# Split SiLU-multiply on one core: each partition owns 128 adjacent rows in place of 8 rows of every block

## The chip, the cores and the metric

The kernel runs on one core of a Trainium2 chip. The metric is device time in microseconds for one execution, the median of several runs.

## The reference

```python
x = np.random.randn(32, 512, 2048).astype(np.float32)

half_dim = x.shape[-1] // 2
x1, x2 = x[..., :half_dim], x[..., half_dim:]
silu_x1 = x1 * (1 / (1 + np.exp(-x1)))
return (silu_x1 * x2).astype(np.float32)      # (32, 512, 1024)
```

There are 32 x 512 = 16,384 rows. A row of x is 2048 floats (8 KB), a row of the output 1024 floats (4 KB). All of x is 134.2 MB, all of the output 67.1 MB.

## The kernel before

The rows are flattened to a 16,384 x 2048 matrix and cut into 16 tiles of 1024 rows. In a tile each of the 128 partitions holds K = 8 rows. Tile i is the i-th block of 1024 adjacent rows; `view` (line 51) cuts it with `"(p k) d -> p k d"`, so partition p holds rows 8p to 8p + 7 of that block. `view` serves the loads (from `x_flat`) and the stores (to `out_flat`) alike.

There are two input buffers `xt` (128 x 8 x 2048) and two output buffers `ot` (128 x 8 x 1024); tile i uses buffer i % 2 of each. For a tile:

- `load(i)` issues one DMA of 8.39 MB from sync's queue (SP; queue q1 in the profile).
- `compute(i)` runs SiLU on the scalar engine (ACT, line 103), in place on the first half of each row in `xt`, and the multiply on the vector engine (DVE, line 109) from `xt` into `ot`. Steady tiles do this in one instruction each over 128 x 8192 elements; tile 0 is cut into four pieces of two rows, the last tile into two pieces of four rows.
- `store(i)` issues one DMA of 4.19 MB from the scalar engine's queue (q10); tile 0 is stored in five pieces that take every fourth or every second partition (`OPENING`), the last tile in two.

All DMAs pass through `move` (line 86), so they carry line 87 in the profile. Loads 0 and 1 go out first. After that the loop issues load i + 2 and the store of tile i in an order that alternates every four tiles (`load_first`); `after` keeps that order without a semaphore wait. Load i + 2 waits for the multiply of tile i, which is the last reader of its buffer; the multiply of tile i waits for the store of tile i - 2, which frees its `ot`. The schedule of ACT and DVE is written out by hand (`manual_schedule`), and `implied` removes dependencies that other waits already cover. At the end sync waits for all the transfers but the last (`settle_all_but`).

Of the kernel before, what the change touches and what calls it, by code (L numbers as in the profile page):

```python
# [1 line left out]

# [4 lines left out]


@with_exitstack
def kernel(  # L10
    ctx: ExitStack,
    tc: tile.TileContext,
    x: bass.AP,
    out: bass.AP,
):


    nc = tc.nc
    P = nc.NUM_PARTITIONS

    x_flat = x.flatten_outer_dims()
    out_flat = out.flatten_outer_dims()
    num_rows, in_cols = x_flat.shape
    half = in_cols // 2
    dt = x_flat.dtype

    K = 8
    KC_EDGE = 2
    KS = 4
    OPENING = [  # L30
        (slice(0, None, 4), slice(0, 2)),
        (slice(2, None, 4), slice(0, 4)),
        (slice(2, None, 4), slice(4, None)),
        (slice(0, None, 4), slice(2, None)),
        (slice(1, None, 2), slice(None)),
    ]
    PLAN = [K] * (num_rows // (P * K))

    pool = ctx.enter_context(tc.tile_pool(name="pool", bufs=1))
    xts = [pool.tile([P, K, in_cols], dt, name=f"xt{b}") for b in range(2)]  # L40
    ots = [pool.tile([P, K, half], dt, name=f"ot{b}") for b in range(2)]

    plan = []
    row = 0
    for k in PLAN:
        plan.append((row, k))
        row += P * k
    assert row == num_rows
    n_tiles = len(plan)

    def view(flat, i):
        row0, k = plan[i]
        return flat[row0:row0 + P * k].rearrange("(p k) d -> p k d", k=k)

    ctx.enter_context(tc.manual_schedule(engines={mybir.EngineType.Activation, mybir.EngineType.DVE}))

    sent = []
    loads, stores, silus, muls = {}, {}, {}, {}

    def implied(later, earlier, reason):  # L60
        for x in later:
            for y in earlier:
                tc.declare_no_dep(x, y, reason=reason)

    def earlier(done, i):
        return [ins for j in range(i % 2, i, 2) for ins in done[j]]

    def after(later, first):
        tc.add_manual_dep(
            later,  # L70
            first.name,
            mybir.DependencyInfo(mybir.DependencyClass.NoSync, mybir.DependencyReason.DATA),
            reason="order in which the transfers take their semaphores",
        )

    def settle_all_but(n):
        rest = nc.sync.nop(nofuse=True)
        for ins in sent[:-n]:
            tc.add_manual_dep(
                rest.ins,  # L80
                ins.name,
                mybir.DependencyInfo(mybir.DependencyClass.Sync, mybir.DependencyReason.DATA),
                reason="sync sees each earlier transfer land before the last ones",
            )

    def move(queue, out, in_):
        ins = queue.dma_start(out=out, in_=in_).ins  # L87
        sent.append(ins)
        return ins

    def load(i):
        loads[i] = [move(nc.sync, xts[i % 2][:], view(x_flat, i))]
        if i >= 2:
            implied(loads[i], earlier(loads, i), "the multiplies that this load awaits came after those loads")
            implied(loads[i], earlier(silus, i), "the multiplies that this load awaits came after those activations")

    def compute(i, ot, kc):
        xt = xts[i % 2]
        silus[i], muls[i] = [], []
        for c in range(0, K, kc):  # L100
            ks = slice(c, c + kc)
            silus[i].append(
                nc.scalar.activation(  # L103
                    out=xt[:, ks, :half],
                    in_=xt[:, ks, :half],
                    func=mybir.ActivationFunctionType.Silu,
                ).ins
            )
            muls[i].append(nc.vector.tensor_mul(out=ot[:, ks], in0=xt[:, ks, :half], in1=xt[:, ks, half:]).ins)  # L109
        implied(muls[i], loads[i], "each multiply awaits an activation that came after the load")  # L110
        if i >= 2:
            implied(silus[i], earlier(silus, i), "the load that this activation awaits came after those activations")
            implied(silus[i], earlier(muls, i), "the load that this activation awaits came after those multiplies")
            implied(muls[i], earlier(muls, i), "the store that this multiply awaits came after those multiplies")

    def store(i, ot, pieces):
        ov = view(out_flat, i)
        stores[i] = [move(nc.scalar, ov[ps, ks], ot[ps, ks]) for ps, ks in pieces]

    ALL = slice(None)  # L120
    load(0)
    load(1)
    for i in range(n_tiles):
        ot = ots[i % 2]
        last = i == n_tiles - 1
        compute(i, ot, KC_EDGE if i == 0 else KS if last else K)
        pieces = [(ALL, ALL)]
        if i == 0:
            pieces = OPENING
        elif last:  # L130
            pieces = [(ALL, slice(c, c + KS)) for c in range(0, K, KS)]
        load_first = i // 4 % 2
        if load_first and i + 2 < n_tiles:
            load(i + 2)
        store(i, ot, pieces)
        if load_first and i + 2 < n_tiles:
            after(stores[i][0], loads[i + 2][0])
        if not load_first and i + 2 < n_tiles:
            load(i + 2)
            after(loads[i + 2][0], stores[i][-1])  # L140
    settle_all_but(1)


# [1 line left out]
_INS = ['x']  # L145
_OUTS = [((32, 512, 1024), 'float32')]


# [23 lines left out]
```

## Time and profile before

| | us |
|---|---|
| median of 3 runs | 470.65 |
| lowest and highest run | 470.65 and 471.86 |
| profiled execution, own time | 471.83 |
| profiled execution, span | 470.1 |
| ACT busy | 114.1 |
| DVE busy | 139.3 |

| transfers | number | MB | median us from issue to landing |
|---|---|---|---|
| loads `xt<-in_x_dram` | 16 | 134.22 | 42.1 |
| whole-tile stores `out_dram<-ot` | 14 | 58.7 | 49.2 |
| pieces of the first and last tile's stores | 7 | 8.4 | 9.4 to 28.1 |

The span is the time from the first to the last instruction of the profiled execution; its own time is the time measured for that same execution as a whole. The profile counts how long the packets of each DMA queue kept the 16 DMA engines busy, as a share of the span. A load in steady state takes 42 us from issue to landing because its packets share the engines with those of a store.

### The profile page before, as it was taken

How to read it: one execution, taken by the hardware profiler on the slowest of the kernel's cores; microseconds unless marked ns; L12 is line 12 of the kernel's file. 1: busy time of each engine (PE TensorE's matmuls, PEld its weight loads, DVE VectorE, ACT ScalarE, POOL GpSimd, SP SyncE). 2: the span in 40 equal slices, each digit the busy share in tenths (PEclk: the TensorE clock that was granted, in tenths of full speed). 3: DMA queues.
4: the chain of work that ended last, by engine and by line, in shares of the span. 5: the costliest groups of instructions: out<-in, count | busy, mean ns of one | idle time of the engine just before them, and what ended most of it. 6: DMA issues, size and time to landing. Idle time of an engine off the chain costs nothing.

```text
span 470.1 us, 157 instructions
## 1 busy us (share of the span) xinstructions
DVE 139.3 (30%) x20; ACT 114.1 (24%) x21; POOL 0.2 (0%) x4
## 2 busy tenths in 40 slices
DVE  0070614307042070520605116060150702507061
ACT  1052305050040501405014050230503205032060
POOL 0000000000000000000000000000000000000000
DMA  8999999999999999999999999999999999999997
GB/s 357 446 468 424 402 441 404 415 480 402 446 402 485 407 421 427 485 407 402 443 446 443 407 443 488 393 415 443 482 407 446 404 429 460 407 446 421 424 425 336
DMA packets 4880, 201.33 MB, mean 428 GB/s; under 512 B 592, under 2 KB 592, under 8 KB 592
## 3 DMA queue, kind: packets, MB, share of 16 engines
q1 hardware_dynamic: 2304, 134.22, 66.2%
q10 hardware_dynamic: 2576, 67.11, 33.1%
HBM read 134.22 MB, written 67.11 MB: 428 GB/s over the span
## 4 chain that ended last, share of the span: by engine, by line
DMA 80%; DVE 14%; ACT 2%; DVEq 1%; issue 0%; SPq 0%
DMA out_dram<-ot 62%; DMA xt<-in_x_dram 18%; DVE ot L109 14%; ACT xt L103 2%; DVEq L167 1%; SPq L87 0%; DVEq L109 0%
## 5 line engine op out<-in xcount | busy, mean ns | idle before, releaser
L109 DVE TENSOR_TENSOR ot<-xt 128x8192 f32<-128x8192 f32 (+2 forms) x20 | 139.3, 6984 | 320.5 <-DMA out_dram<-ot 180.1
L103 ACT ACTIVATE xt<-xt 128x8192 f32<-128x8192 f32 (+2 forms) x20 | 112.8, 5661 | 339.7 <-DMA xt<-in_x_dram 339.7
L103 ACT ACT_TABLE_LOAD x1 | 1.3, 1283 | 0.7 <-PEq L156 0.7
L156 POOL MEMSET const-bfloat16-1.0<- 128x1 bf16 x1 | 0.1, 102 | 0.0
L156 POOL MEMSET const-uint8-127<- 128x1 uint8 x1 | 0.1, 102 | 0.0
L156 POOL MEMSET const-float32-0.0<- 128x1 f32 x1 | 0.1, 99 | 0.2 <-issue 0.2
L156 POOL MEMSET const-float32-1.0<- 128x1 f32 x1 | 0.1, 99 | 0.0
## 6 DMA issues: line engine op xcount, KB each, us to landing
out_dram<-ot ACTq DMA_DIRECT2D x14, 4096.0 KB, 49.2
out_dram<-ot ACTq DMA_DIRECT2D x3, 2048.0 KB, 9.4
out_dram<-ot ACTq DMA_DIRECT2D x2, 512.0 KB, 17.3
out_dram<-ot ACTq DMA_DIRECT2D x1, 768.0 KB, 28.1
xt<-in_x_dram SPq DMA_DIRECT2D x16, 42.1
out_dram<-ot ACTq DMA_DIRECT2D x1, 256.0 KB, 10.9
```

Of the source, the lines that this page charges most:

```text
L103: nc.scalar.activation(out=xt[:, ks, :half], in_=xt[:, ks, :half], func=mybir.ActivationFunctionType.Silu,).ins
L109: muls[i].append(nc.vector.tensor_mul(out=ot[:, ks], in0=xt[:, ks, :half], in1=xt[:, ks, half:]).ins)
L156: nc = _bacc.Bacc("TRN2", target_bir_lowering=False, num_devices=1)
L167: with _tile.TileContext(nc) as tc:
```

## The change

Partition p now owns rows 128p to 128p + 127 of x and of the output, and tile i is the i-th group of eight rows of each partition. The tiles keep their shape, number and order, and eight adjacent rows still go to a partition in each tile. The list `plan` falls away, since the new view needs only the tile's number.

```diff
-    PLAN = [K] * (num_rows // (P * K))
+    n_tiles = num_rows // (P * K)
...
-    plan = []
-    row = 0
-    for k in PLAN:
-        plan.append((row, k))
-        row += P * k
-    assert row == num_rows
-    n_tiles = len(plan)
-
     def view(flat, i):
-        row0, k = plan[i]
-        return flat[row0:row0 + P * k].rearrange("(p k) d -> p k d", k=k)
+        return flat.rearrange("(p t k) d -> t p k d", p=P, k=K)[i]
```

Rows of x that one partition reads for tile i:

| | first row | bytes in one run | from one partition's run to the next partition's | from a tile to the next, same partition |
|---|---|---|---|---|
| before, x | 1024 i + 8 p | 64 KiB | 64 KiB | 8 MiB |
| after, x | 128 p + 8 i | 64 KiB | 1 MiB | 64 KiB |
| before, out | 1024 i + 8 p | 32 KiB | 32 KiB | 4 MiB |
| after, out | 128 p + 8 i | 32 KiB | 512 KiB | 32 KiB |

## The prediction

> **What bounds the kernel now.** I read the page from the top: busy shares, then the DMA queues, then the chain that ended last, then the waits, and last the work in stretches of one steady length.
>
> ```profile
> span 470.1 us, 157 instructions
> DVE 139.3 (30%) x20; ACT 114.1 (24%) x21; POOL 0.2 (0%) x4
> DMA packets 4880, 201.33 MB, mean 428 GB/s; under 512 B 592, under 2 KB 592, under 8 KB 592
> q1 hardware_dynamic: 2304, 134.22, 66.2%
> q10 hardware_dynamic: 2576, 67.11, 33.1%
> DMA out_dram<-ot 62%; DMA xt<-in_x_dram 18%; DVE ot L109 14%; ACT xt L103 2%; DVEq L167 1%; SPq L87 0%; DVEq L109 0%
> ```
>
> No compute engine is busy for a third of the span. The two queues (q1 the loads, q10 the stores) together take 66.2 + 33.1 = 99.3% of all 16 DMA engines' time, and the chain is 80% DMA. The chain names the stores most often only because each multiply waits for its `ot` buffer; the engines under it also carry the loads.
>
> The queue lines give a price per byte. Loads: 0.662 x 470.1 = 311.2 us for 134.22 MB, or 431 GB/s. Stores: 0.331 x 470.1 = 155.6 us for 67.11 MB, also 431 GB/s. They give the packet size too. There are 16 loads and 21 stores, and 37 x 16 engines = 592, the number of packets under 512 B, so these are the small ones that end each transfer. Of the 2304 on q1, 256 are such, and 2048 carry data: 134.22 MB / 2048 = 65,536 B. One load is 128 packets, one for each partition's eight adjacent rows. A packet takes at most 16 x 311.2 us / 2048 = 2.43 us.
>
> The stretches show how steady this is. Columns: the stretch and its length, busy time on DVE, ACT and POOL, the granted clock, the DMA share, GB/s.
>
> ```profile
> 0.00:60.00 60.00, 17.52 (x5) 15.62 (x6) 0.20 (x4) 1.00 0.99 419
> 60.00:118.00 58.00, 17.45 (x3) 14.06 (x2) 0.00 (x0) 1.00 0.99 425
> 118.00:176.00 58.00, 17.39 (x2) 14.06 (x2) 0.00 (x0) 1.00 1.00 434
> ...
> 350.00:408.00 58.00, 17.38 (x2) 14.06 (x2) 0.00 (x0) 1.00 1.00 434
> 408.00:470.10 62.10, 17.45 (x3) 14.15 (x3) 0.00 (x0) 1.00 0.96 414
> ```
>
> Two tiles (25.17 MB) pass in each 58 us, at 434 GB/s and a share of 1.00. Only the start and the drain are lower. The waits show the slack on the other side:
>
> ```profile
> ACT xt L103 <- DMA xt<-in_x_dram: 339.7, 16, 22.4
> DVE ot L109 <- DMA out_dram<-ot: 180.1, 9, 20.8
> DVE ot L109 <- ACT xt L103: 140.4, 7, 24.6
> ```
>
> ACT waits about 22 us for each load, DVE about 20 us for a store or for ACT. Nothing that shortens compute could help, and anything that lengthens a packet lengthens the span almost one for one, since the engines have 0.7% idle to give.
>
> **What the change removes and adds: addresses only.** The list `plan` is Python and costs no instruction. Loads stay 16 and stores 21; the SBUF side, the semaphores, the order of issue and all ACT and DVE work stay as they are. A partition still reads 8 x 8 KB = 64 KiB in one run and writes 8 x 4 KB = 32 KiB in one run, so I expect the 4880 packets again. All this costs nothing, with no cover needed.
>
> What moves is where the runs lie in memory. In x, neighbouring partitions lie 64 KiB apart before and 128 rows x 8 KB = 1 MiB apart after; in out, 32 KiB before and 512 KiB after. A tile was one solid block of 8 MiB of x; it becomes 128 islands over the whole 128 MiB, and the next tile is the next 64 KiB of each. So the addresses that the 16 engines have in flight at one moment now differ by whole multiples of 1 MiB (512 KiB for stores). Whether the memory serves such addresses at 434 GB/s is the whole question, and no row of before has a pitch over 64 KiB.
>
> **Bounds from the trace.** The good end: 434 GB/s is a rate that does not move through five stretches, and loads and stores share it, so a better memory layout has little to give. What it could give stands in the stretches at the start: 60 x (1 - 419/434) = 2.1 us, and 58 x (1 - 425/434) = 1.2 us, together -3.3 us. (The drain at the end, 414 GB/s, waits for compute on the last tile and has no layout in it.)
>
> The bad end has to come from the lowest rates that any row holds with both queues at work. These two answers are for shorter stretches:
>
> ```profile
> 32.00:40.00 8.00, 1.47 (x1) 0.00 (x0) 0.00 (x0) 1.00 0.83 342
> 60.00:72.00 12.00, 0.07 (x1) 2.00 (x1) 0.00 (x0) 1.00 0.94 393
> 72.00:84.00 12.00, 6.84 (x1) 5.03 (x1) 0.00 (x0) 1.00 1.11 481
> ```
>
> They are poor witnesses: 393 is followed by 481 at a share over 1, so part of the dip is packets booked in the next stretch. I use them only as distances: 434/393 = 1.104, 434/342 = 1.27. Applied to the loads' 311.2 us they are +32.5 us and +83.7 us; applied to the stores' 155.6 us, 393 is +16.2 us.
>
> I take +32.5 us, on the loads alone: 393 is the nearer of the low rows to the steady 434, and the loads carry two thirds of the bytes and twice the stores' pitch. Ends kept for the range: -3.3 us and +83.7 us, with the stores' 16.2 us on top.
>
> One rule speaks against the change. The row first: before, at a pitch of 64 KiB and 32 KiB, both queues move 431 GB/s. The Trainium skill, "DMA: Bandwidth & Descriptors", section "Latency and other measured facts", says that copies between HBM tensors of 128 x 16 KiB tiles slow down when the partitions' rows lie a large power of two apart: 214 GB/s each way at full rate, 207 at 512 KiB, 164 at 2 MiB, 103 at 4 MiB; it calls the cause, aliasing of the partitions' streams, an inference. By that page, as an estimate, the stores would cost 155.6 x (214/207 - 1) = +5.3 us and the loads, between its 512 KiB and 2 MiB, +10.5 to +94.9 us, so 486 to 571 us. Those copies have HBM on both ends and these transfers have SBUF on one; no row here shows such a pitch.
>
> **Sum.** The profiled execution took 471.83 us: 470.1 us of span and 1.7 us around it. That is 1.2 us above the median of 470.65 of the runs shown. With loads at 393 GB/s: 471.8 + 32.5 = 504.3, less 1.2 to stand at the median: 503 us. The stall then sits in the loads. ACT waits longer for each, about 32.5/16 = 2 us per tile; DVE and the stores behind it follow two us later per tile, and nothing else becomes late, because ACT (114 us busy) and DVE (139 us) have over 300 us of idle time.
>
> **The rivals.**
> 1. The memory has room and the engines hide the new addresses: no change, 470.7 us. For it: loads and stores run at the very same 431 GB/s although one reads and the other writes, which looks like a limit of the engines and not of the memory, and 64 KiB in one run is long. Against it: nothing says how much room there is, and the new pitch is 16 times the old one.
> 2. The wide pitch slows both queues hard: loads at 342, stores at 393. 470.65 + 83.7 + 16.2 = 570.6 us. For it: loads and stores both get a pitch of a power of two, and they are in flight together all the time. Against it: the stores' pitch is half as wide, and the 342 row lies at the change from the opening pieces to the steady order.
> 3. Faster, by one mechanism: runs far apart disturb each other less than neighbours do, at the place where the rows are below 434, the first 118 us. Price -3.3 us: 467.4 us. It decides only if loads and stores of the later stretches stay at 434, and it cannot go further because the share there is already 1.00.
> That the change doesn't do what it says: if the new view did not merge eight rows into one run, packets would be 8 KB and eight times as many. The eight rows are adjacent in both views, so I give this nothing of its own.
>
> **How the numbers follow.** A measurement of this kernel can tell about 0.3%, 1.4 us, from no change. Loads slowed, 503 us, with its own range from 480 to 530: 0.55. No change, 469.3 to 472: 0.22. Both queues slowed, about 571: 0.17. Faster, 467: 0.06. So slower is 0.55 + 0.17 = 0.72. The low end of the range is the low end of the case without change, 469.3, since that case must be held; the high end is 560, which is loads at 342 alone (554) and a little of the stores. Left out are the faster case (0.06) and about two thirds of the hard one (0.11).
>
> **What the profile after would show.** Right: 4880 packets and 201.33 MB again; the steady stretches of 58 us near 400 GB/s in place of 434 with the share still near 1.00; q1's share of the span up from 66.2% (343.7 us of 503 is 68%); ACT's wait for loads up by about 30 us; the same busy time on ACT and DVE. If q10's share grows as much as q1's, the stores suffer too. If the steady stretches still say 434, the memory hid it and the time is 470.7 within 1.4 us. If the packets are not 4880, the runs were cut differently and the whole sum is void.
>
> What would make this wrong is above all that the price of the pitch is taken from rows that do not contain it: its sign is fairly safe, as the steady share of 1.00 leaves no room for a gain, and its size is not.

## The result, and the profile after

The changed kernel took 487.72 us (median of 6 runs, 484.31 to 490.19), against 470.71 us before (470.65 to 471.93). The ratio is 1.035, 95% interval 1.033 to 1.038: slower by 17 us. The new times scatter over 6 us where the old ones scatter over 1.3.

The profiled execution took 487.92 us, its span 486.1. The page first (busy shares, packets, the two queues):

```profile
span 486.1 us, 157 instructions
DVE 139.4 (29%) x20; ACT 114.1 (23%) x21; POOL 0.2 (0%) x4
GB/s 340 350 390 341 325 363 394 415 423 439 431 445 418 429 442 429 442 426 437 431 426 437 439 429 429 426 437 437 448 415 439 437 429 437 429 434 442 410 377 299
DMA packets 4880, 201.33 MB, mean 414 GB/s; under 512 B 592, under 2 KB 592, under 8 KB 592
q1 hardware_dynamic: 2304, 134.22, 66.6%
q10 hardware_dynamic: 2576, 67.11, 32.0%
```

Compute and packets are what they were. The loads now take 0.666 x 486.1 = 323.7 us of the 16 engines, 12.5 us more than before; the stores 0.320 x 486.1 = 155.6 us, the same as before. And the row of GB/s says where: seven slices of 12 us at the start are low, then it is the old rate.

The stretches of the changed kernel, same columns as in the prediction:

```profile
0.00:60.00 60.00, 8.90 (x4) 13.31 (x6) 0.20 (x4) 1.00 0.98 353
60.00:118.00 58.00, 17.39 (x2) 13.04 (x3) 0.00 (x0) 1.00 0.99 400
118.00:176.00 58.00, 17.38 (x2) 13.70 (x3) 0.00 (x0) 1.00 1.00 434
...
350.00:408.00 58.00, 17.39 (x2) 14.05 (x3) 0.00 (x0) 1.00 1.00 432
408.00:486.10 78.10, 26.15 (x4) 18.57 (x4) 0.00 (x0) 1.00 0.93 402
```

The 16.0 us between the spans can be counted from these. The first 60 us: 60 x (419 - 353)/434 = 9.1. The next 58: 58 x (425 - 400)/434 = 3.3. The five middle stretches read 434, 434, 432, 433, 432 against 434 five times: 58 x 5/434 = 0.7. The drain: 78.1 x (1 - 402/434) = 5.8 against 62.1 x (1 - 414/434) = 2.9 before, so 2.9 more. Together 16.0. The share of busy engines is near 1.00 in the low stretches at the start: the engines are not idle, their packets take longer. In the drain the share is lower instead (0.93 against 0.96): some engines are done while others still work.

One more view shows what kind of state that is. It is the DMA page of a 24 us window, 130 to 154 us, in 40 slices of 0.6 us; packets are booked in one slice each, so a row shows when the 16 engines turn over. Before:

```profile
GB/s 819 0 1693 0 109 0 1638 0 109 0 765 55 1584 109 109 0 765 55 1584 109 109 0 765 55 1584 109 109 0 765 55 1584 109 109 0 655 164 1256 437 109 0
```

After:

```profile
GB/s 765 164 492 328 382 492 765 164 492 328 382 492 601 109 655 437 492 218 437 546 655 273 492 328 437 655 492 164 328 655 437 382 382 437 273 601 492 437 382 437
```

Both windows lie in stretches at 434 GB/s. Before, nearly all of the 16 engines begin their packets in the same 0.6 us: the rate jumps between 0 and about 1600. That is called in step here. After, once the slow start is over, packets begin at all times: the engines are out of step. The trace's packet records say the same: the 16 engines end their share of a load within 0.6 us of each other at load 0 and 1.4 us at load 15 before; after, within 1.8 us at load 0, 5.8 at load 1 and 6.6 at load 15.

### The profile page after: what moved, and what is told of

The parts are those of the page before. It is cut to its first block, busy times and chain, and to the rows that moved or that the text cites. A ratio compares the mean times of both kernels' runs of the same rounds, so it can differ in the third digit from the quotient of the medians.

```text
span 486.1 us, 157 instructions
## 1 busy us (share of the span) xinstructions
DVE 139.4 (29%) x20; ACT 114.1 (23%) x21; POOL 0.2 (0%) x4
## 2 busy tenths in 40 slices
DMA packets 4880, 201.33 MB, mean 414 GB/s; under 512 B 592, under 2 KB 592, under 8 KB 592
## 4 chain that ended last, share of the span: by engine, by line
DMA 73%; DVE 15%; another core or an unknown queue 8%; ACT 1%; DVEq 1%; issue 0%; ACTq 0%
DMA out_dram<-ot 59%; DVE ot L100 15%; DMA xt<-in_x_dram 14%; ACT xt L94 1%; DVEq L158 1%; ACTq L78 0%; DVEq L100 0%
## 5 line engine op out<-in xcount | busy, mean ns | idle before, releaser
L94 ACT ACTIVATE xt<-xt 128x8192 f32<-128x8192 f32 (+2 forms) x20 | 112.8, 5661 | 355.8 <-DMA xt<-in_x_dram 355.8
```

Source lines behind the costliest of these rows:

```text
L94: nc.scalar.activation(out=xt[:, ks, :half], in_=xt[:, ks, :half], func=mybir.ActivationFunctionType.Silu,).ins
```

## The experiments

The runs below test one theory against its rivals. **Theory A**: the 16 engines run in step, so with a pitch of 1 MiB they read at one moment from addresses that differ by whole multiples of 1 MiB. Those reads disturb each other, which delays some engines more than others, until the delays have put them out of step; from then on the full rate is back, and what stays is the spread of the engines, paid at the drain. **Rivals**: B, a wide spread of addresses is slow by itself at the start of the program; C, the stores' pitch does it; D, each entry into the wide pitch is paid anew.

### Which queue pays: loads alone, stores alone

```diff
+    def near(flat, i):
+        return flat[i * P * K:(i + 1) * P * K].rearrange("(p k) d -> p k d", k=K)
+    def far(flat, i):
+        return flat.rearrange("(p t k) d -> t p k d", p=P, k=K)[i]
     def view(flat, i):
-        return flat.rearrange("(p t k) d -> t p k d", p=P, k=K)[i]
+        return (far if flat is x_flat else near)(flat, i)      # loads_far; stores_far: the other way round
```

> Only the loads use the new rows; the stores keep the old ones, so the output's rows are permuted. Theory A (the loads pay: the 16 engines start in step on addresses that differ by multiples of 1 MiB, disturb each other until the delays have pushed them out of step, then run at full rate): 484 to 490 us, the first 60 us near 353 GB/s, later stretches 434. Rival theory C (the stores at a 512 KiB pitch start it or keep it going): near 471 us, or about halfway, 479.

> Only the stores use the new rows; the loads keep the old ones, so the output's rows are permuted. Theory A: 470 to 472 us, with 434 GB/s in the steady stretches. Rival theory C: 478 us or more, with the loss in the stretches after 30 us, when the stores begin.

Loads alone: 483.22 us, ratio 1.025 (1.020 to 1.031). Stores alone: 474.44 us, 1.007 (1.004 to 1.010). The sum of the two losses, 12.5 + 3.7 = 16.2 us, is nearly the 17.0 of the whole change. Theory A's number for the loads was a little high (484 to 490, and 353 GB/s in the first 60 us, where 370 came) and its zero for the stores was wrong; C, that the stores start it, falls by its size. Stretches with new rows in the loads only:

```profile
0.00:60.00 60.00, 9.97 (x5) 15.62 (x6) 0.20 (x4) 1.00 0.98 370
60.00:118.00 58.00, 18.43 (x3) 14.06 (x2) 0.00 (x0) 1.00 1.00 428
408.00:480.10 72.10, 24.80 (x4) 14.15 (x3) 0.00 (x0) 1.00 0.92 397
```

and with new rows in the stores only:

```profile
0.00:60.00 60.00, 17.55 (x5) 15.62 (x6) 0.20 (x4) 1.00 0.99 419
118.00:176.00 58.00, 17.38 (x2) 14.06 (x2) 0.00 (x0) 1.00 1.00 432
408.00:473.00 65.00, 17.80 (x4) 14.15 (x3) 0.00 (x0) 1.00 0.92 398
```

The loads carry the slow start. The stores hardly slow anything while the kernel runs; most of their cost is in the last row, 65 x (1 - 398/434) = 5.4 us of drain against 2.9 before. In that run the engines end the last load within 4.3 us of each other, against 1.4.

### Wide or a power of two: 960 KiB, 512 KiB, 256 KiB, and 1 MiB less 8 KiB

```diff
+    T = 15                                     # also 8 and 4
     def view(flat, i):
-        return flat.rearrange("(p t k) d -> t p k d", p=P, k=K)[i]
+        first = i // T * T
+        t = min(T, n_tiles - first)
+        rows = flat[first * P * K:(first + t) * P * K]
+        return rows.rearrange("(p t k) d -> t p k d", p=P, k=K)[i - first]
```

> Each partition owns 120 adjacent rows for tiles 0 to 14 (pitch 960 KiB in x, 480 KiB in out, not a power of two); tile 15 is the block of the last 1024 rows as before. Theory A, in which equal low address bits over a power of two matter: 470 to 473 us, no slow start. Rival theory B (a wide pitch is slow by itself at the start, since the reads are spread over the whole of x): 484 us or more, as with 1 MiB.

> Two halves of eight tiles; within each, a partition owns 64 adjacent rows (pitch 512 KiB in x, 256 KiB in out). Theory A: a smaller loss than with 1 MiB, 473 to 483 us, all of it in the first 120 us, as the engines stay out of step for the second half. Theory B: like A at the start, but the loss comes back at tile 8, near 290 us, when the reads move to new places.

> Four groups of four tiles; within each a partition owns 32 adjacent rows (pitch 256 KiB in x, 128 KiB in out). Theory A with a loss that grows with the power of two: between the kernel before (64 KiB) and 512 KiB, 470.5 to 474 us. Theory B (only the spread over memory counts): the same range; this run fills in the curve.

The last one keeps the new rows for the stores and takes 127 in place of 128 rows from one partition's loads to the next:

```diff
     def view(flat, i):
-        return flat.rearrange("(p t k) d -> t p k d", p=P, k=K)[i]
+        if flat is not x_flat:
+            return flat.rearrange("(p t k) d -> t p k d", p=P, k=K)[i]
+        each = 127
+        rows = flat[:P * each].rearrange("(p r) d -> p r d", p=P)
+        if (i + 1) * K <= each:
+            return rows[:, i * K:(i + 1) * K]
+        return rows[:, each - K:]
```

> The loads' pitch is 127 rows, 1 MiB less 8 KiB, and the stores keep the new pitch of 512 KiB (some rows of x are read by two partitions and some by none, so the output is not the reference's). Theory A (addresses a whole power of two apart collide): the loads' loss of 12.5 us goes, the stores' 3.7 us stays, so 472 to 477 us. Theory B (spread over the whole of x): 484 to 490 us.

| loads' pitch | stores' pitch | us | ratio to before, interval |
|---|---|---|---|
| 64 KiB (before) | 32 KiB | 470.7 | |
| 256 KiB | 128 KiB | 472.80 | 1.0036 (1.0025 to 1.0047) |
| 512 KiB | 256 KiB | 474.07 | 1.0056 (1.0034 to 1.0078) |
| 960 KiB | 480 KiB | 471.41 | 1.0006 (0.9986 to 1.0026) |
| 1016 KiB | 512 KiB | 474.30 | 1.0060 (1.0039 to 1.0082) |
| 1 MiB | 32 KiB (loads alone) | 483.22 | 1.0252 (1.0197 to 1.0306) |
| 1 MiB | 512 KiB (the change) | 487.72 | 1.0352 (1.0326 to 1.0377) |

960 KiB spreads the reads over almost as much memory as 1 MiB and can't be told from the kernel before: B falls. In its trace the engines are in step all along (between 130 and 154 us a load packet has on average 13.3 other load packets starting within 0.3 us of it) and its middle stretches read 434. With 1016 KiB for the loads, what is left is 474.30 us, what the stores alone cost (474.44). Taking 8 KiB, 0.8%, off the pitch of the loads takes away all of their 12.5 us. The start of that run:

```profile
0.00:60.00 60.00, 17.59 (x5) 15.62 (x6) 0.20 (x4) 1.00 0.99 419
60.00:118.00 58.00, 17.39 (x2) 14.06 (x2) 0.00 (x0) 1.00 0.99 424
```

Among powers of two the loss grows with the pitch, little up to 512 KiB and steeply at 1 MiB. One part of theory A's forecast for 512 KiB missed: the loss was not in the first 120 us, where the rows say 419 and 422 against 419 and 425 before, but mostly in the drain, 63.6 x (1 - 407/434) = 4.0 us against 2.9. Its engines are out of step too, their ends 3.2 us apart from load 3 on. So engines can go out of step with no slow start.

### When it is paid: wide pitch late, or early

```diff
-        return flat.rearrange("(p t k) d -> t p k d", p=P, k=K)[i]
+        return (far if i >= 8 else near)(flat, i)     # late;  early: far if i < 4
```

> Tiles 0 to 7 use the old rows, tiles 8 to 15 the new ones, loads and stores (the output is not the reference's: rows of the second half are served twice or not at all). Theory A (engines in step collide wherever the 1 MiB pitch begins): the loss appears when load 8 starts, near 205 us, in the stretches from 176 to 292 us, and the first 118 us are as before; 477 to 490 us. Rival theory B (the loss belongs to the start of the program and not to the state of the engines): 470 to 472 us.

> Tiles 0 to 3 use the new rows, tiles 4 to 15 the old ones (the output is not the reference's). Theory A: the whole loss of the change, 483 to 489 us, since it falls in the first 100 us; the later stretches at 434. If instead the loss of about 16 us were a small share of every tile, a quarter of it would be left, 475 us.

The two runs took 487.63 us (late) and 486.76 us (early); but these times can't be used whole. Where stores change from one layout to the other they write rows that an earlier store wrote, and the program makes them wait for it: with new rows in tiles 0 to 3, the store after the multiply that ends at 157.1 us is issued only at 177.6. So I take from the early run its first 118 us (357 and 412 GB/s against 353 and 400 in the changed kernel), and repeated the other with the layout changed in the loads alone, which is loads against loads:

```diff
-        return (far if i >= 8 else near)(flat, i)
+        return (far if flat is x_flat and i >= 8 else near)(flat, i)              # late2
+        return (far if flat is x_flat and not 4 <= i < 10 else near)(flat, i)     # twice
```

> As the run with the new rows from tile 8 on, but only the loads change; all stores keep the old rows, so that no store overlaps an earlier one's rows and waits for it (the output is not the reference's). Theory A: the first 176 us as before, the loss from load 8 on, near 205 us; at most the 12.5 us that the loads cost alone, 476 to 484. Rival theory B (the start of the program): 470 to 472 us.

> Only the loads change: new rows in tiles 0 to 3, old rows in 4 to 9, new rows again in 10 to 15 (the output is not the reference's). Theory A (the loss is paid once, until the engines are out of step, and they stay so): 480 to 486 us, as with new rows in all loads, and the stretches after 240 us at 430 or more. Rival theory D (each change to the wide pitch is paid anew, or old rows bring the engines back into step): 488 us or more, with a second dip after 250 us.

Late: 480.82 us, 1.021 (1.019 to 1.023). Twice: 484.49 us, 1.028 (1.025 to 1.031), against 483.22 with the wide pitch in all loads. The stretches of one tile each (29 us), wide pitch from load 8 on, which is issued at 201.3 us:

```profile
147.00:176.00 29.00, 8.69 (x1) 7.03 (x1) 0.00 (x0) 1.00 1.00 434
176.00:205.00 29.00, 8.69 (x1) 7.03 (x1) 0.00 (x0) 1.00 1.00 434
205.00:234.00 29.00, 8.69 (x1) 7.03 (x1) 0.00 (x0) 1.00 1.07 375
234.00:263.00 29.00, 3.88 (x1) 7.03 (x1) 0.00 (x0) 1.00 0.97 405
263.00:292.00 29.00, 8.39 (x2) 7.03 (x1) 0.00 (x0) 1.00 1.01 432
```

So the start of the program has no part in it: the dip comes where the pitch comes, in the middle of the steady pattern, and is over after two tiles. (It begins some 12 us behind the issue, since load 7, ahead of load 8 on the same queue, lands only at 214.1 us. In the kernel before, too, about 13 of a load's 42 us from issue to landing pass behind the load ahead of it.) The same stretches of the run that enters the wide pitch a second time, at load 10, issued at 271.8 us:

```profile
234.00:263.00 29.00, 8.69 (x1) 7.03 (x1) 0.00 (x0) 1.00 1.00 434
263.00:292.00 29.00, 8.69 (x1) 7.03 (x1) 0.00 (x0) 1.00 1.00 432
292.00:321.00 29.00, 8.69 (x1) 7.03 (x1) 0.00 (x0) 1.00 1.00 432
321.00:350.00 29.00, 8.69 (x1) 6.94 (x1) 0.00 (x0) 1.00 1.00 434
```

The same entry, from old rows into new ones, costs 0.3 us here and cost 5.9 us there. One thing that differs is the state of the engines, in the 24 us windows just ahead of each entry, in slices of 0.6 us: wide pitch late (180 to 204 us), then twice (240 to 264 us).

```profile
GB/s 55 1638 109 0 0 819 55 819 55 1638 109 0 0 710 164 1311 437 0 0 1311 437 0 0 655 218 1311 437 0 0 655 218 1311 437 0 0 655 218 1311 437 0
```

```profile
GB/s 492 655 218 492 437 328 492 655 218 492 382 382 382 655 328 492 273 328 492 601 273 328 546 437 328 546 382 546 437 492 328 437 546 546 218 437 382 546 437 382
```

With the engines in step the entry is paid; with the engines out of step from the first payment it is not, and six tiles of old rows did not bring them back into step. D falls. The part of theory A that says where the loss begins has its support here, though not alone: the two entries also differ in which of load and store is issued first at those tiles, and in the second run the loads had been at the wide pitch before. Nothing was run to take these apart.

The part of theory A that says why the loss ends is not shown, and the traces speak against it. In the changed kernel the engines are soon out of step while the loads are still slow. This is its window from 60 to 84 us, again in slices of 0.6 us, at a mean of 365 GB/s:

```profile
GB/s 109 355 874 437 0 0 150 287 928 451 437 109 205 191 628 382 341 546 328 478 109 218 655 109 164 328 382 601 273 382 546 273 328 273 492 601 218 437 437 546
```

The packet records say it more sharply. Between 20 and 30 us a load packet has on average 3.9 other load packets starting within 0.3 us of it (11.2 before), between 40 and 50 us 3.2, and from 118 to 400 us, at full rate, 2.6. Yet load packets take 2.81 us on average in the first of these windows and 3.35 us in the second, against 2.43 us in the third: the loss is greatest when the step is already gone.

The run with loads and stores both changed from tile 8 on shows the same from the other side. After its dip near 205 us and the wait of a store it has a second dip, with the engines out of step (2.5 load packets within 0.3 us), no new change of pitch and the DMA share at 1.00:

```profile
292.00:350.00 58.00, 17.38 (x2) 17.75 (x3) 0.00 (x0) 1.00 1.00 401
```

So being in step is not what the loss needs in order to last. Whether a finer alignment of the engines than the starts of their packets decides it, no run here shows.

### Two attempts to put the engines out of step by other means

> The changed kernel, with 15 small extra loads first on the scalar engine's queue: of 15 partitions, then 14, down to 1, each 4 KB per partition, into an output buffer that is overwritten later. They add 0.49 MB, 1.1 us at 434 GB/s, and give the DMA engines unequal work at the start, so that they are out of step early. Theory A: most of the loss goes, 472 to 480 us, the first 60 us above 400 GB/s. Theory B, and any theory in which the 1 MiB pitch costs a fixed amount: 485 to 490 us.

> The changed kernel with five small extra loads on the scalar engine's queue right after load 0 is issued, each into rows of its own of the second input buffer, which load 1 overwrites: of 13, 10, 8, 5 and 2 partitions, 8 KB each, 0.31 MB in all, 0.7 us at 434 GB/s. They give some DMA engines more work than others in the first 20 us and wait for nothing. Theory A: the engines are pushed out of step sooner, so the loss shrinks, 474 to 484 us. If out of step by so little is not enough, or if the loss has another cause: 485 to 491 us.

```diff
     ALL = slice(None)
+    for k in range(15, 0, -1):                                             # stagger
+        nc.scalar.dma_start(out=ots[1][:k, 0, :], in_=x_flat[:k, :half])
     load(0)
+    for j, k in enumerate((13, 10, 8, 5, 2)):                              # stagger2, in place of the other
+        nc.scalar.dma_start(out=xts[1][:k, j], in_=x_flat[:k])
```

Both failed, and neither answers its question. The first took 523.53 us: the 15 loads share one destination, so each waited for the one before, and while loads 0 and 1 were in flight they followed each other 7 to 11 us apart; the scalar engine was held until 69 us, and the row of GB/s fell to 12 and 46 GB/s in two slices. The second took 508.31 us: its small loads landed only with load 0, so load 1, which overwrites them, was issued at 29.2 us and the order of the whole kernel shifted.

One row of the second speaks against theory A's account of the end once more:

```profile
118.00:176.00 58.00, 17.39 (x2) 14.06 (x2) 0.00 (x0) 1.00 1.00 421
```

Its stretches stay between 421 and 425 from there to the end, although its engines end a load 5 to 8 us apart by then. In that order of loads and stores, being out of step isn't enough for the full rate. Why is open.

## Why the prediction was right or wrong

**Direction and range: right.** Slower was given 0.72; 487.7 lies between 469.3 and 560, and in the likeliest case's own 480 to 530, but near its low end: of the forecast loss of 32.5 us half came.

**Bound by the DMA engines, compute far off the path: right.** Packets 4880 again, ACT and DVE busy as before. The wait of ACT for loads went from 339.7 to 355.8, by the 16 us that the span grew and not by the forecast 30:

```profile
ACT xt L94 <- DMA xt<-in_x_dram: 355.8, 16, 24.6
```

**The loads pay, the stores' packets don't: right in kind.** The loads' queue grew by 12.5 us, the stores' by nothing.

**The step that failed is the size of the loads' term, and the reason is its form.** The sum let every load run at 393 GB/s from the first to the last, +32.5 us. The runs show loads held back for an episode, about 90 us here and two tiles in the run with the loads' late entry; then the rows say 432 to 434 again. The forecast "steady stretches near 400" was wrong. In the sum's own terms the loads were +12.5 us of engine time. The price of 393 was itself not far off for the time in which it applied (353 in the first 60 us, 400 in the next 58); the stretch in which it applied was a fifth of what the sum gave it. Why the episode ends stays open. That the time still fell into the range owes something to luck: too long a stretch was partly made up for by the width of the range, and nothing in the prediction said that the loss would stop.

**A term was missing:** the drain, +2.9 us. The prediction said that the drain has no layout in it, and that was wrong. Over the runs without a stall it goes roughly with how far apart the engines end the last load: 2.9 us of drain at 1.4 us apart (before), 3.6 at 2.2 (256 KiB), 4.0 at 3.6 (512 KiB), 5.4 at 4.3 (stores alone), 5.8 at 6.6 (the change). That the spread causes it is likely but was not tested by itself. The stores' cost (3.7 us alone) is mostly of this kind; the prediction had it at nothing in its likeliest case.

**The rivals.** "No change" had the best argument for the steady state, and there it was right: the engines' limit does hide the new addresses from 118 us on. It overlooked the way there. "Both queues hard" found no support: no row of the changed kernel's steady part is below 432. "Faster" would have needed the first 118 us to improve; they carry the loss.

The Trainium skill ("DMA: Bandwidth & Descriptors", section "Latency and other measured facts") has the rule that pitches of a large power of two slow copies between HBM tensors and that a few KiB of padding restore the rate. The loads here agree in both: 1 MiB costs them 12.5 us, and with 8 KiB less none of that is left. Its 512 KiB figure for all the run, the low end of the prediction's estimate by that page, would have been 486; that this is near 487.7 is chance, since here the loads at 1 MiB lose for a fifth of the time and hardly anything after.

## What to carry to other kernels

When 128 partitions stream from addresses a large power of two apart, look at the first tiles and at the drain, not at the steady rate: the mean hides a start that is 16% slow (353 GB/s against 419) and an end in which engines finish apart. If a partition must own a long stretch, choose a pitch that is no power of two; for the loads 960 KiB and 1016 KiB were free of it where 1 MiB wasn't. And ask how long such a loss can last before pricing it over all the bytes: here it ended by itself after a fifth of the time, for a reason that the runs leave open.

## What the runs showed of the hardware

The 16 DMA engines stayed in step for the whole of the kernel before (their ends 0.6 us apart at load 0, 1.4 us at load 15) and with a pitch of 960 KiB, and six tiles of the old rows did not bring them back into step once they were out. Out of step costs no rate by itself: at 512 KiB the middle stretches read 434. The loss of the loads at a pitch of 1 MiB is here not a steady rate but an episode: 374 GB/s in the changed kernel from 6 to 30 us, where hardly anything but loads is in flight, against 437 before, and 432 to 434 at the same pitch from 118 to 408 us. It is not always a single one, as the second dip to 401 GB/s and the 421 to 425 GB/s of the run with five small extra loads show. No kernel that was run beats the one before; 960 KiB, at 471.41 us, is the only layout that can't be told from it.
